# Convolution with max pooling: the input rows of four image pairs as bfloat16 by casting DMA, their row sums by two-input addition, two row differences on VectorE

## The chip, the cores and the metric

The kernel runs on one core of one Trainium2 chip. The metric is the device time of one launch in microseconds. Three runs of the kernel before took 105.48, 104.73 and 104.98 us; the median is 104.98.

A core has five engines that run their own instruction streams and wait for one another by semaphores: TensorE (PE, matrix products, with its weight loads as PEld), VectorE (DVE), ScalarE (ACT), GpSimd (POOL) and SyncE (SP, which here only issues DMAs). SBUF is the working memory of 128 partitions; PSUM is the memory that TensorE writes, here eight banks, each a tile `acc` of 128 x 512 float32.

## What is computed

A convolution of 16 images (64 channels, 64 x 64) with a 3 x 3 kernel to 128 channels, zero padding of one, then the maximum over 2 x 2 windows:

```python
x_pad = np.pad(x, ((0, 0), (0, 0), (pad, pad), (pad, pad)), mode='constant')
...
conv[b, co] += weight[co, ci, kh, kw] * x_pad[b, ci, kh:kh+h, kw:kw+w]
...
output[b, c, i, j] = np.max(conv[b, c, i*pool_size:(i+1)*pool_size,
                                      j*pool_size:(j+1)*pool_size])
```

## The kernel before

**Tiles and steps.** Two images lie side by side on the partitions (64 channels each), so there are eight image pairs. A pair is cut into four quarters of 16 rows (8 rows after pooling), which makes 32 steps. Each step is done for both halves, that is for both images; every TensorE operation has a partner on the other half of the array, and the two run side by side. The string `TYPES` gives each step its kind. Steps of kind K (11 of them) read the rows as bfloat16, with five products: two for each of the two output rows of a pooling window, and one on the sum of two input rows (`ks`), which both output rows have in common and which is added after the maximum of the two. Steps of kind W (21) first transform the rows into a row difference `wd` (16 rows), a row difference `we` and a row sum `ws` (8 rows each), and are left with four products; the one on `ws` is added after the row maximum. `place` gives each step its pair and quarter; with the K steps first, steps 3, 4, 6, 8 are the quarters of pair 3, steps 9, 11, 12, 14 those of pair 4, 16, 17, 19, 20 those of pair 5, 22 to 25 those of pair 6 and 27, 28, 30, 31 those of pair 7.

**Operations.** In the order list an operation is named by letters, step and, where it has one, half:
- loads: `L` and `LB` (float32 rows of a W step into one of three tiles `wx`, issued on SP; `LB` also waits for the last two-input operation of VectorE), `LK` (rows of K steps into `kx`, cast to bfloat16 by the DMA, issued on POOL)
- row operations: `KS` (sum for a K step, VectorE), `WS` (`ws`, VectorE), `E` (`we`, POOL, or VectorE for four steps), `D` (`wd`, POOL)
- products on TensorE: `PA1`, `PA2`, `PB1`, `PB2`, `PR` for K steps, `P2` (reads `we`), `P0` and `P3` (read `wd`), `P1` (reads `ws`) for W steps. A product is three matmuls of 512 or 504 columns.
- after the products: `EV` (ScalarE copies the first bank out), `SE` (ScalarE copies it into the second bank), `MX` (rowmax, VectorE), `OD` (ScalarE copies the odd columns), `CM` (colmax, VectorE, which frees the second bank), and then the store on SP.
- at the start: preparation of the weights (`GS`, `GM`, `uGM`, `TGM` and others like them: sums on POOL and VectorE, copies on POOL, transposes on TensorE) and casts of the first K rows (`XOa`, `XEb`, `X1`).

**What sets the order.** The schedule is written out by hand: the text `ORDER` (line 493) lists every operation, and each engine runs its own in that order. Products of the two halves wait in two lanes and are issued in pairs. One rule is added: an operation of POOL (`on_gpsimd`) waits for the last two-input operation on SBUF that VectorE has before it in the order (`on_vector`). `WS` is a two-input addition under that rule, except for the steps in `SUM_BY_REDUCTION` (line 40), where it is a reduction over pairs of rows (line 315) that isn't noted by `on_vector`.

**What the change touches.** `wload` (97) and `late_load` (390) for the loads, `wx_rows` (306) for the tile that a W step reads, `ws` (310) and `wd` (337) for the sums and the 16-row difference. The order list stays the same, among it these parts:

```
... TG1 GS F.2.0 VD2 XOa LB.3 LB.4 LB.6 LB.8 LB.9 GM VG0 F.3.0 XOb F.0.0 uGM ... XEb LK.0.0 ...
... E.11 P1.6.0 D.11 ... WS.9 ... KS.10 ... E.14 ... D.14 E.12 ... WS.11 ... D.12 L.22 L.23 ... D.16 ... WS.14 ...
... WS.16 ... D.17 ... E.17 D.20 E.20 D.19 ... WS.17 ...
```

Of the kernel before, what the change touches and what calls it, by code (L numbers as in the profile page):

```python
# [11 lines left out]
def kernel(  # L12
# [9 lines left out]
    nc = tc.nc  # L22
    FP32 = mybir.dt.float32
    BF16 = mybir.dt.bfloat16
    MAX = mybir.AluOpType.max
    ADD = mybir.AluOpType.add
    SUB = mybir.AluOpType.subtract

    B, CI, H, W = x.shape
# [4 lines left out]
    R = HO // NQ  # L34
# [2 lines left out]
    TYPES = "KWKWWKWKWWKWWKWKWWKWWKWWWWKWWKWW"  # L37
    DIFF_ON_VECTOR = (3, 4, 6, 11,)
    CAST_ON_VECTOR = ()
    SUM_BY_REDUCTION = (1, 3, 9, 11, 12, 14, 16, 17, 19, 20, 22,)  # L40
    N = len(TYPES)
    KSTEPS = [s for s in range(N) if TYPES[s] == "K"]
    WSTEPS = [s for s in range(N) if TYPES[s] == "W"]
# [4 lines left out]
    const = ctx.enter_context(tc.tile_pool(name="const", bufs=1))  # L48
# [18 lines left out]
    sbuf_op = [None]  # L67

    def behind(inst, other):
        if other is not None:  # L70
            tc.add_manual_dep(inst.ins, other.ins.name, SYNC, reason="order")
# [5 lines left out]
    def on_gpsimd(inst):  # L77
        behind(inst, sbuf_op[0])
        return inst


    def rows_of(p, lo, hi):
        return x[2 * p : 2 * p + 2].rearrange("b c h w -> (b c) h w")[:, lo:hi, :]

    def chunk(q):
        return (2 * R * q + (q > 0), min(H, 2 * R * (q + 1) + 1))

    NWX = 3
    kx = {}
    wx = [const.tile([128, H + 2, W], FP32, name=f"wx_{i}") for i in range(NWX)]  # L90

    def kload(p, lo, hi):
        if p not in kx:
            kx[p] = kx_pool.tile([128, H, W], BF16, name="kx")
        return nc.gpsimd.dma_start(out=kx[p][:, lo:hi, :], in_=rows_of(p, lo, hi))  # L95

    def wload(s, part=None):
        p, q = place[s]
        lo, hi = chunk(q)
        if s == WSTEPS[0] and q > 0:  # L100
            lo = 2 * R * q - 1
        if part == 0:
            hi = 2 * R * q + R + 1
        elif part == 1:
            lo = 2 * R * q + R + 1
        return nc.sync.dma_start(out=wx[p % NWX][:, lo + 1 : hi + 1, :], in_=rows_of(p, lo, hi))
# [11 lines left out]
    for s in first_loads:  # L118
        if s == KSTEPS[1]:
            nc.sync.dma_start(out=ksecond, in_=rows_of(0, klo2, khi2))  # L120
        else:
            wload(s, 0)
            wload(s, 1)
# [2 lines left out]
    ident = const.tile([128, 128], BF16)  # L126
    make_identity(nc, ident)
    for t in wx:
        nc.gpsimd.memset(t[:, 0, :], 0.0)
        nc.gpsimd.memset(t[:, H + 1, :], 0.0)  # L130

# [163 lines left out]
    row = {}  # L295
# [9 lines left out]

    def wx_rows(s):
        p, q = place[s]
        return wx[p % NWX], 2 * R * q + 1

    def ws(s):  # L310
        row["ws", s] = ws_pool.tile([128, R, W], BF16, name="ws")
        t, f = wx_rows(s)
        if s in SUM_BY_REDUCTION:
            with nc.allow_low_precision("bf16 operand of TensorE, as the other row sums"):
                nc.vector.tensor_reduce(  # L315
                    out=row["ws", s],
                    in_=t[:, f : f + 2 * R, :].rearrange("p (r two) w -> p r w two", two=2),
                    axis=mybir.AxisListType.X,
                    op=ADD,
                )  # L320
            return
        on_vector(
            nc.vector.tensor_tensor(  # L323
                out=row["ws", s], in0=t[:, f : f + 2 * R : 2, :], in1=t[:, f + 1 : f + 2 * R : 2, :], op=ADD
            )
        )

    def we(s):
        row["we", s] = e_pool.tile([128, R, W], BF16, name="we")
        t, f = wx_rows(s)  # L330
        vector = s in DIFF_ON_VECTOR
        inst = (nc.vector if vector else nc.gpsimd).tensor_tensor(  # L332
            out=row["we", s], in0=t[:, f : f + 2 * R : 2, :], in1=t[:, f + 1 : f + 2 * R : 2, :], op=SUB
        )
        (on_vector if vector else on_gpsimd)(inst)

    def wd(s):
        row["wd", s] = d_pool.tile([128, 2 * R, W], BF16, name="wd")
        t, f = wx_rows(s)
        on_gpsimd(  # L340
            nc.gpsimd.tensor_tensor(  # L341
                out=row["wd", s], in0=t[:, f + 1 : f + 1 + 2 * R, :], in1=t[:, f - 1 : f - 1 + 2 * R, :], op=SUB
            )
        )

    def we_half(part):
        s = WSTEPS[0]
        if part == 0:
            row["we", s] = e_pool.tile([128, R, W], BF16, name="we")
        t, f = wx_rows(s)  # L350
        lo, hi = f + R * part, f + R * (part + 1)
        on_vector(
            nc.vector.tensor_tensor(
                out=row["we", s][:, R // 2 * part : R // 2 * (part + 1), :],
                in0=t[:, lo:hi:2, :],
                in1=t[:, lo + 1 : hi : 2, :],
                op=SUB,
            )
        )
# [16 lines left out]
    def lk(n, part):  # L376
        quarters = min(NQ, NK - n * NQ)
        last = min(H, 2 * R * quarters + 1)
        half = 2 * R * 2 + 1
        if n == 0:  # L380
            inst = kload(0, *chunk(2 + part))
            if part == 0:
                behind(inst, sbuf_op[0])
        elif part == 0:
            kload(n, 0, min(last, half))
        else:
            kload(n, half, last)


    def late_load(s):  # L390
        behind(wload(s), sbuf_op[0])

    ev, od, ot, made = {}, {}, {}, {}

# [58 lines left out]
    def cast_more(first):  # L453
# [27 lines left out]
        "SEa": lambda h: seed_half(0, h),  # L481
        "SEb": lambda h: seed_half(1, h),
        "KS": ks, "WS": ws, "E": we, "D": wd, "L": wload, "LB": late_load, "LK": lk,
        "SE": seed, "EV": evac, "MX": rowmax, "OD": odd, "CM": colmax,
    }
# [108 lines left out]
```

## Time and profile before

The profiled execution has a span of 103.4 us from its first to its last instruction; the page gives no other time of that execution. The mean granted clock of TensorE is 0.993.

| | before |
|---|---|
| median of three runs | 104.98 us |
| span of the profiled execution | 103.4 us |
| ScalarE busy | 82.2 us (79%) |
| `wd` on POOL, line 341 | 20 of 2.36 us |
| `we` on POOL, line 332 | 16 of 1.27 us |
| `ws` by reduction, line 315 | 11 of 1.23 us |
| `ws` by two-input addition on float32, line 323 | 10 of 0.72 us |
| `ks`, two-input addition on bfloat16, line 301 | 11 of 0.43 us |
| casting loads issued on POOL, line 95 | 6 of 0.59 us |
| moved by DMA | 23.33 MB, 226 GB/s on average |

A row of the timeline gives the start in us from the beginning of the span, the duration, the engine, the line of the kernel, the operation, the tiles as written<-read with their shapes, and in brackets how long the engine had been idle before it and what ended that.

### The profile page before, as it was taken

How to read it: one execution, taken by the hardware profiler on the slowest of the kernel's cores; microseconds unless marked ns; L12 is line 12 of the kernel's file. 1: busy time of each engine (PE TensorE's matmuls, PEld its weight loads, DVE VectorE, ACT ScalarE, POOL GpSimd, SP SyncE). 2: the span in 40 equal slices, each digit the busy share in tenths (PEclk: the TensorE clock that was granted, in tenths of full speed). 3: DMA queues.
4: the chain of work that ended last, by engine and by line, in shares of the span. 5: the costliest groups of instructions: out<-in, count | busy, mean ns of one | idle time of the engine just before them, and what ended most of it. 6: DMA issues, size and time to landing. Idle time of an engine off the chain costs nothing.

```text
span 103.4 us, 2541 instructions
## 1 busy us (share of the span) xinstructions
PE 97.2 (94%) x909; PEld 62.9 (61%) x909; DVE 92.0 (89%) x179; ACT 82.2 (79%) x181; POOL 75.6 (73%) x65
## 2 busy tenths in 40 slices
PE   6999799999999999999999999999999999999910
PEld 2497655555865465576666685556746777777600
DVE  1389899999999999999999999999989996979960
ACT  4546988886789997993887898987899898698820
POOL 6046869773995899998999997959997919970000
PEclk9999999999999999999999999999999999999997
DMA  2988999999999999999859992187699232006152
GB/s 62 299 312 262 360 291 268 349 416 404 248 194 298 286 318 339 351 340 204 163 159 261 312 384 101 56 205 263 176 154 257 81 136 101 0 13 233 65 202 102
DMA packets 13341, 23.33 MB, mean 226 GB/s; under 512 B 1040, under 2 KB 9488, under 8 KB 13328
## 3 DMA queue, kind: packets, MB, share of 16 engines
q1 hardware_dynamic: 12320, 20.68, 60.8%
q0 software_dynamic: 864, 2.36, 13.7%
q8 instruction: 7, 0.11, 0.4%
q10 hardware_dynamic: 144, 0.13, 0.4%
q14 instruction: 6, 0.05, 0.1%
HBM read 17.14 MB, written 8.39 MB: 247 GB/s over the span
## 4 chain that ended last, share of the span: by engine, by line
PE 91%; DVE 3%; issue 1%; DVEq 0%
PE acc L200 85%; PE acc L551 3%; PE acc L164 2%; DVE acc L427 2%; DVE o L437 1%; DVEq L589 0%; DVEq L437 0%; DVEq L427 0%
## 5 line engine op out<-in xcount | busy, mean ns | idle before, releaser
L200 PEld LDWEIGHTS <-wt 64*128 64x128 bf16 x876 | 59.6, 94 | 31.5 <-issue 1.5
L341 POOL TENSOR_TENSOR wd<-wx 128x1024 bf16<-128x1024 f32 x20 | 47.1, 2361 | 7.7 <-PE acc L200 3.4
L200 PE MATMUL acc<-wd,wt 64*128 64x504 bf16 (+3 forms) x264 | 50.1, 367 | 0.0
L200 PE MATMUL acc<-kx,wt 64*128 64x504 bf16 (+6 forms) x288 | 50.0, 356 | 0.0
L427 DVE TENSOR_TENSOR acc<-acc,ev 128x512 f32<-128x512 f32 x64 | 42.0, 691 | 1.1 <-ACT ev L401 0.3
L200 PE MATMUL acc<-we,wt 64*128 64x512 bf16 (+2 forms) x132 | 31.7, 367 | 0.0
L200 PE MATMUL acc<-ws,wt 64*128 64x504 bf16 (+1 forms) x126 | 28.7, 377 | 0.1
L401 ACT ACTIVATE ev<-acc 128x512 f32<-128x512 f32 x42 | 25.1, 608 | 2.7 <-PE acc L200 2.3
L431 ACT COPY od<-acc 128x256 f32<-128x256 f32 x64 | 22.5, 379 | 5.8 <-PE acc L200 5.2
L437 DVE TENSOR_TENSOR o<-acc,od 128x256 f32<-128x256 f32 x64 | 24.5, 416 | 2.1 <-ACT od L431 1.9
L411 ACT COPY acc<-acc 128x512 f32<-128x512 f32 x40 | 23.0, 581 | 3.0 <-PE acc L200 1.7
L332 POOL TENSOR_TENSOR we<-wx 128x512 bf16<-128x512 f32 x16 | 20.2, 1273 | 3.3 <-DVE ws L323 2.4
L200 PE MATMUL acc<-ks,wt 64*128 64x504 bf16 (+1 forms) x66 | 16.5, 377 | 0.5 <-DVE acc L427 0.5
L315 DVE TENSOR_REDUCE ws<-wx 128x512 bf16<-128x1024 f32 x11 | 13.5, 1229 | 0.0
L399 ACT COPY ev<-acc 128x512 f32<-128x512 f32 x22 | 12.9, 595 | 0.6 <-PE acc L200 0.6
L323 DVE TENSOR_TENSOR ws<-wx 128x512 bf16<-128x512 f32 x10 | 7.1, 723 | 0.0
L301 DVE TENSOR_TENSOR ks<-kx 128x512 bf16<-128x512 bf16 x11 | 4.6, 429 | 0.3 <-ACT kx L458 0.3
L551 PE MATMUL acc<-const-bfloat16-1.0 128*128 128x512 bf16 x8 | 3.6, 628 | 0.8 <-PEq L575 0.8
L95 POOL DMA_DIRECT2D kx<-in_x_dram x6 | 3.5, 587 | 0.7 <-DVE kx L451 0.7
L164 PEld LDWEIGHTS <-wq 128*128 128x128 bf16 x25 | 2.3, 132 | 1.4 <-issue 1.4
L151 POOL COPY wq<-wq 128x64 bf16<-128x64 bf16 x3 | 0.7, 241 | 3.1 <-ACT wq L462 2.5
L164 PE MATMUL acc<-ident,wq 128*128 128x128 bf16 x25 | 2.8, 285 | 0.0
(30 smaller groups left out, 22.3 us busy)
## 6 DMA issues: line engine op xcount, KB each, us to landing
out_dram<-o SPq DMA_DIRECT2D x31, 256.0 KB, 4.2
wx<-in_x_dram SPq DMA_DIRECT2D x10, 512.0 KB, 7.2
wx<-in_x_dram SPq DMA_DIRECT2D x5, 544.0 KB, 7.6
wx<-in_x_dram SPq DMA_DIRECT2D x5, 480.0 KB, 7.4
kx<-in_x_dram POOLq DMA_DIRECT2D x2, 528.0 KB, 7.4
ksecond<-in_x_dram SPq DMA_DIRECT2D x1, 512.0 KB, 7.0
kx<-in_x_dram POOLq DMA_DIRECT2D x2, 256.0 KB, 7.0
kx<-in_x_dram POOLq DMA_DIRECT2D x1, 496.0 KB, 12.0
```

The costliest lines, as they stand in the source:

```text
L164: nc.tensor.transpose(tp[:, (j - lo) * CO : (j - lo + 1) * CO], wq[:, j : j + 2, :].rearrange("a b c -> a (b c)"), ident,)
L200: nc.tensor.matmul(acc[t][:, i0:i1, o0:o1], wt[lo : lo + CI, tap_of(m0, kw, h), :], rows(lo, i0, i1, c0, c1), start=start and kw == 1, sto ...
L315: nc.vector.tensor_reduce(out=row["ws", s], in_=t[:, f : f + 2 * R, :].rearrange("p (r two) w -> p r w two", two=2), axis=mybir.AxisListTy ...
L323: nc.vector.tensor_tensor(out=row["ws", s], in0=t[:, f : f + 2 * R : 2, :], in1=t[:, f + 1 : f + 2 * R : 2, :], op=ADD)
L332: inst = (nc.vector if vector else nc.gpsimd).tensor_tensor(out=row["we", s], in0=t[:, f : f + 2 * R : 2, :], in1=t[:, f + 1 : f + 2 * R : ...
L341: nc.gpsimd.tensor_tensor(out=row["wd", s], in0=t[:, f + 1 : f + 1 + 2 * R, :], in1=t[:, f - 1 : f - 1 + 2 * R, :], op=SUB)
L399: nc.scalar.copy(out=ev[s, h], in_=acc[t])
L401: nc.scalar.mul(ev[s, h], acc[t], -1.0)
L411: nc.scalar.copy(out=acc[t], in_=acc[ta[s, h]])
L427: nc.vector.tensor_tensor(out=t, in0=t, in1=ev[s, h], op=MAX)
L431: nc.scalar.copy(out=od[s, h], in_=acc[tb[s, h]][:, :, 1::2])
L437: nc.vector.tensor_tensor(out=ot[s][:, h], in0=acc[t][:, :, 0::2], in1=od[s, h], op=MAX)
```

## The change

The W steps of pairs 4 to 7 read their rows from four new bfloat16 tiles `wb`, one for each pair, instead of the three float32 tiles `wx`. Two quarters are loaded at once, by one casting DMA on POOL's queue, where the first of the two stands in the order list; the second's entry in the list does nothing. So sixteen loads on SP become eight on POOL: those of `LB.9`, `L.12`, `L.16`, `L.19`, `L.22`, `L.24`, `L.27` and `L.30`. Two rows of each new tile are zeroed at the start by POOL. The nine row sums of these pairs that were reductions become two-input additions, noted by `on_vector`; the two of pair 2 and pair 3 (steps 1 and 3) stay reductions. The 16-row differences of steps 12 and 19 move from POOL to VectorE, at their places in the list.

```diff
-    SUM_BY_REDUCTION = (1, 3, 9, 11, 12, 14, 16, 17, 19, 20, 22,)
+    SUM_BY_REDUCTION = (1, 3,)
+    TAPS_ON_VECTOR = (12, 19,)
+    FIRST_BF16 = 4
...
+    wb = {
+        p: const.tile([128, H + 2, W], BF16, name=f"wb_{p}") for p in range(FIRST_BF16, B // 2)
+    }
...
     def wload(s, part=None):
         p, q = place[s]
+        if p in wb:
+            if q % 2:
+                return None
+            lo, hi = chunk(q)[0], chunk(q + 1)[1]
+            return nc.gpsimd.dma_start(out=wb[p][:, lo + 1 : hi + 1, :], in_=rows_of(p, lo, hi))
...
+    for t in wb.values():
+        nc.gpsimd.memset(t[:, 0, :], 0.0)
+        nc.gpsimd.memset(t[:, H + 1, :], 0.0)
...
     def wx_rows(s):
         p, q = place[s]
-        return wx[p % NWX], 2 * R * q + 1
+        return wb.get(p, wx[p % NWX]), 2 * R * q + 1
...
     def wd(s):
         row["wd", s] = d_pool.tile([128, 2 * R, W], BF16, name="wd")
         t, f = wx_rows(s)
-        on_gpsimd(
-            nc.gpsimd.tensor_tensor(
-                out=row["wd", s], in0=t[:, f + 1 : f + 1 + 2 * R, :], in1=t[:, f - 1 : f - 1 + 2 * R, :], op=SUB
-            )
+        vector = s in TAPS_ON_VECTOR
+        inst = (nc.vector if vector else nc.gpsimd).tensor_tensor(
+            out=row["wd", s], in0=t[:, f + 1 : f + 1 + 2 * R, :], in1=t[:, f - 1 : f - 1 + 2 * R, :], op=SUB
         )
+        (on_vector if vector else on_gpsimd)(inst)
...
     def late_load(s):
-        behind(wload(s), sbuf_op[0])
+        inst = wload(s)
+        if inst is not None:
+            behind(inst, sbuf_op[0])
```

## The prediction

> **What bounds the kernel now.** I read the busy shares first, then the chain of waits, then the table by stretches of time, and last the timelines of VectorE (DVE), GpSimd (POOL), TensorE (PE) and the DMA issues around each step that the change touches.
>
> ```profile
> PE 97.2 (94%) x909; PEld 62.9 (61%) x909; DVE 92.0 (89%) x179; ACT 82.2 (79%) x181; POOL 75.6 (73%) x65
> PE 91%; DVE 3%; issue 1%; DVEq 0%
> 11.03 64.89 PE acc L200 x609
> 75.94 20.43 PE acc L200 x186
> 40.00:50.00 10.00, 10.00 (x96) 6.50 (x93) 10.00 (x18) 7.62 (x18) 9.50 (x7) 1.00 0.97 289
> ```
>
> The chain of waits is TensorE alone from 11.03 to 96.37: 795 matmuls in 85.3 us, two side by side every 0.215 us, at a granted clock of 1.00. In the last row (PE, PEld, DVE, ACT, POOL busy, then clock, DMA share, GB/s) VectorE is as full as TensorE, and the DMA engines are full too. So less work on VectorE wins nothing by itself, while anything that reaches TensorE late is paid in full. And the order was cut close: colmax CM.9.1 ends at 39.33 and the matmul that needs its PSUM bank starts at 39.45; D.3 ends at 16.16 and its first matmul starts at 16.25. Through the middle the bank that a colmax frees is taken up 0.05 to 0.7 us later, again and again (end of each colmax in VectorE's timeline against the start of the matmul that the bank order gives it).
>
> **The change, part by part.**
>
> *VectorE's own work falls.* Nine reductions of 1.23 us (L315) become two-input sums on bfloat16; the nearest row is L301, the same shape on bfloat16, at 0.43: 9 x 0.80 = 7.2 us. The seven two-input sums on the bfloat16 pairs go from 0.68 to 0.43: 1.8 us. D.12 and D.19 come to VectorE: twice the elements of L301's 0.43. L437 with 256 elements takes 0.42 and L332 with 512 takes 0.68, so 512 more cost up to 0.53 in f32, or half of that if bfloat16 runs at twice the rate, as L301 against L332 suggests: 0.70 to 0.96 each. I take 0.70, the row of the same type. Net -7.6 us of 92.0. At nothing for the end, since TensorE is full.
>
> *POOL* loses two operations of 2.36 us (L341), gains eight DMA issues at 0.54 to 0.70 (L95), some 4.6 us, and eight memsets at the start, which run every 0.09 us: 0.7 us, covered by its wait of 2.52 us at 4.79. Whether its operations get shorter on bfloat16 no row shows; between 2.36 and half of it, I take 2.36. SP loses sixteen loads.
>
> *Where the sums meet POOL.* This is the first cost. The timelines of the two engines show what happens when a VectorE operation with two SBUF inputs is issued while POOL runs one:
>
> ```profile
> 67.76 1.27 POOL L332 TENSOR_TENSOR we<-wx 128x512 bf16<-128x512 f32 x1 [0.51 <-DVE ks L301]
> 68.72 0.87 DVE L323 TENSOR_TENSOR ws<-wx 128x512 bf16<-128x512 f32 x1
> 69.67 4.68 POOL L341 TENSOR_TENSOR wd<-wx 128x1024 bf16<-128x1024 f32 x2 [0.63 <-DVE ws L323]
> 74.03 0.86 DVE L323 TENSOR_TENSOR ws<-wx 128x512 bf16<-128x512 f32 x1
> 37.78 1.23 DVE L315 TENSOR_REDUCE ws<-wx 128x512 bf16<-128x1024 f32 x1
> ```
>
> The sum at 68.72 ends 0.56 after POOL's operation (69.03), the one at 74.03 ends 0.54 after it (74.35), L301's at 67.03 0.28 after it (67.25): VectorE stands still until POOL is done, then streams (0.55 us in f32, 0.28 in bfloat16). The reduction at 37.78 runs under a POOL operation (37.09 to 39.46) at its usual 1.23. So a sum that now falls under POOL's operation waits for that operation's end, and VectorE's queue behind it (rowmax, colmax, which free PSUM banks) waits too. On the other side, POOL's operations are ordered behind the last two-input VectorE operation, so each new one adds a wait to POOL. In the times of before:
> - WS.9 (34.16): D.11 holds POOL to 35.45; end 35.73 for 35.39, 0.34 late.
> - WS.11: E.14 started 0.25 later behind KS.10, D.14 ends at 39.70, the sum at 39.98 for 39.00: 1.0 late. CM.9.1 is next and had 0.11: TensorE stands 0.9.
> - D.12 adds 0.6 to VectorE: 1.6 late. D.16 now waits for it, 42.1 to 44.45. WS.14 comes at 42.75 and ends at 44.73 for 42.34: 2.4 late. WS.12 meets no operation and wins back 0.8. Colmax CM.10.1, whose bank had 0.24, is 1.6 late: TensorE's loss is 1.4.
> - WS.16 wins 0.8 back, but D.17 waits for it: 50.5 for 47.54. So E.17 ends at 54.1 and D.20 follows. D.19, at VectorE's turn at 54.0, waits for E.17, ends at 54.7; WS.17 right behind it waits for D.20 (54.7 to 57.05) and ends at 57.35 for 54.27: 3.1 late. The next colmax, CM.13.0, had 0.28: TensorE's loss is 2.8.
> - From WS.20 on the sums are short, POOL no longer has D.19, and VectorE catches up; TensorE can't.
>
> Who goes first when POOL has a second operation queued (E.12 behind D.14, D.20 behind E.17) no row shows: always VectorE gives 1.4, always POOL about 4.1 (WS.17 at 58.7). I take 2.8, the alternation.
>
> *The loads at the start.* This is the second cost. Today pair 4's first rows are LB.9, the last of five loads issued on SP from 6.95. The change makes them one casting load of 33 rows, twice as large, on POOL's queue ahead of LK.0.0: after gsum, 6.77 to about 7.4. uGM then starts at 7.45 for 7.40, which the transposes at 8.12 hide.
>
> ```profile
> q1 hardware_dynamic: 12320, 20.68, 60.8%
> q0 software_dynamic: 864, 2.36, 13.7%
> 8.00:13.00 5.00, 4.46 (x71) 3.40 (x69) 4.59 (x10) 4.19 (x11) 3.97 (x5) 1.00 0.94 312
> 13.00:20.00 7.00, 7.00 (x70) 3.68 (x66) 6.79 (x13) 6.17 (x15) 5.44 (x3) 1.00 1.06 294
> 13.02 0.69 DVE L332 TENSOR_TENSOR we<-wx 128x512 bf16<-128x512 f32 x1
> 13.80 4.67 POOL L341 TENSOR_TENSOR wd<-wx 128x1024 bf16<-128x1024 f32 x2 [1.14 <-DVE we L332]
> 16.25 0.38 PE L200 MATMUL acc<-wd,wt 64*128 64x512 bf16 x1
> ```
>
> The casting queue's 2.36 MB are bfloat16, so 4.72 MB read, in 13.7% of 16 x 103.4 us: 48 us of one DMA engine for each MB, as for the plain queue (48.6). So casting saves no DMA time, and the 1.08 MB of this load take 1.08 x 48 / 16 = 3.2 us of all engines, in a stretch whose DMA share is 0.94 to 1.06. Two steps wait there. LB.3, issued at 6.95, landed 6.0 later at 12.95, and E.3 reads it at 13.02; D.3 follows, and its matmul at 16.25 had 0.09. LB.3 comes later by between 0 (the older load wins) and 3.2 (the new load goes between); issued within half a microsecond of each other, I take the half, 1.6: TensorE stands 1.5. LK.0.0, now behind the new load in one queue, landed 9.0 after 8.32, at 17.3, for the matmuls at 18.21; later by 0 to 3.2, I take 2.4, since all of the new load is ahead of it: 19.7, also 1.5 after its need. The two don't add, since a stand at 16.25 moves 18.21 as well. LK.0.1 (12.09 + 8.4 = 20.5, used at 20.6) moves with them. LK.0.0 today, issued by 9.02, landed behind LB.4 (7.32 + 7.1 = 14.4) though LB.4 was long under way, which speaks for something near the order of issue. The Trainium skill (DMA: Bandwidth & Descriptors, Queues, rings and completion order) says that a DMA engine takes turns between its queues, packet by packet. By that LB.3 would bear nearly the whole 3.2 and the sum would be 1.6 higher, as in the last rival below.
>
> Later casting loads are needed over 10 us after their issue, and stores that wait beside them hold output tiles, of which there are six; both at nothing. A step takes TensorE 85.3 / 32 = 2.7 us, so a tile comes round after 16 us, and a store that took 8 more than its median of 4.2 would still be in time.
>
> *Sum.* 1.5 + 2.8 = 4.3 us on the profiled execution's span of 103.4. The page gives that execution no time of its own; the median of the runs, 104.98, is 1.6 us above its span, and I leave these 1.6 as they are: 109.3.
>
> **The rivals.**
> - *One of the two costs is hidden.* For it: the new load may queue behind LB.3, or VectorE may get its turn each time. Against: both spots have under 0.3 us. It gives 104.98 + 1.5 to 2.8: 106.5 to 107.8. A POOL that runs bfloat16 in half the time belongs here: D.14 and D.20 then hold VectorE 1.2 us less, leaving about 1 us in the middle: 107.5. The Trainium skill (GPSIMD Engine Reference, Elementwise — side-by-side cycle accounting) counts cycles for each element, not byte, which would keep 2.36; no row here can show it.
> - *VectorE's 7.6 us cover it all, not slower.* Sums with their 0.8 us won run ahead of POOL instead of under it, and loads land in the order of issue. It decides if VectorE is nowhere over 0.3 us late at a colmax: 105.0. Against: the first sums, WS.9 and WS.11, fall under POOL operations that are already running, before anything is won.
> - *Faster by over 1%.* It would need TensorE to save more than the 0.54 us that it idles at 11.03 and the 1.1 of issue in the chain: about 104. Nothing in the change shortens a matmul.
> - *Every turn goes to POOL and the new load goes first*: 3.1 + 4.1: 112.2.
>
> **How the numbers follow.** This kernel can tell about 1% from no change. Both costs 0.45; one hidden 0.27; all hidden 0.12; faster 0.04; every turn to POOL 0.12. Slower is 0.45 + 0.27 + 0.12 = 0.84. The range leaves out the worst of the last case and most of the two that are not slower: 105.4 to 112.2.
>
> **What would show it.** Right: a wait of TensorE between 14 and 21 us that ends with wd or kx, E.3 starting after 14; sums at L323 of 1 to 3 us instead of 0.43 where POOL runs; POOL waiting for ws more often than its five times now. Wrong: TensorE's row of busy x96 in every ten microseconds as before, the sums all at 0.43, the reads of pair 3 landing by 13.0.

## The result and the profile after

| | before | after |
|---|---|---|
| median of the runs on the same chip | 105.05 us (104.73 to 105.48, 4 runs) | 110.73 us (109.57 to 111.59, 4 runs) |
| ratio, 95% interval | | 1.053 [1.044, 1.061] |
| span of the profiled execution | 103.4 us | 109.8 us |

The change makes the kernel slower by 5.7 us. The profiled execution of after took 111.59 us, the longest of its four; its steps are therefore compared below with those of other kernels that contain the same parts.

Busy shares and the chain of waits (share of the span by engine), from the page of after:

```profile
PE 97.7 (89%) x909; PEld 57.2 (52%) x909; DVE 90.3 (82%) x181; ACT 81.9 (75%) x181; POOL 71.9 (65%) x79
PE 46%; DVE 5%; issue 1%; ACT 1%; DVEq 0%; ACTq 0%
```

TensorE does the same 909 matmuls in nearly the same 97.7 us, in a span 6.4 us longer. The chain that ended last is no longer TensorE from end to end. Its pieces in order of time (start, us, what), from 47.46 on:

```profile
47.46 0.58 ACT acc L427
...
48.08 11.84 PE acc L214 x107
...
59.96 0.27 DVE ws L337
...
60.85 0.70 DVE acc L443
...
61.59 39.09 PE acc L214 x358
```

TensorE's row is broken twice, by ScalarE's copy into a bank at 47.46 and by a row sum and a rowmax of VectorE at 60. The waits of TensorE (total us, times, longest) name a third place:

```profile
PE acc L214 <- DMA kx<-in_x_dram: 3.1, 1, 3.1
PE acc L214 <- DVE acc L443: 2.2, 2, 1.6
PE acc L214 <- ACT acc L427: 1.1, 1, 1.1
```

To size these places I set the start of each product matmul of after against the same matmul of before. The lateness grows at three matmuls only (each growth is counted from the level that it had after the one before), and by the last matmul (98.30 before, 104.55 after) it is 6.25 us:

| matmul | before | after | lateness grows by | what it waits for |
|---|---|---|---|---|
| PA1.5, first half | 18.21 | 21.32 | 3.3 (from 0.17 early) | LK.0.0, landed at 21.27 |
| P0.12, second half | 43.38 | 48.08 | 1.59 | SE.12 on ScalarE, which waited for a colmax queued behind WS.14 |
| PR.15, second half | 55.06 | 61.59 | 1.83 | MX.15.1 on VectorE, queued behind D.19 and WS.17 |

The last two in the stretches of time (us, busy time and count of PE, PEld, DVE, ACT, POOL, then clock, DMA share, GB/s):

```profile
44.00:48.00 4.00, 2.94 (x27) 1.21 (x24) 4.00 (x8) 2.19 (x6) 2.64 (x2) 1.00 0.87 105
56.00:62.00 6.00, 4.38 (x42) 2.76 (x39) 5.60 (x8) 3.68 (x8) 5.49 (x4) 1.00 0.72 183
```

TensorE works 2.94 of four and 4.38 of six microseconds there. VectorE counts as busy almost throughout, as before; how much of that is standing still, only the durations show. The timeline of POOL and VectorE around the two places:

```profile
39.87 2.12 POOL L355 TENSOR_TENSOR wd<-wb 128x1024 bf16<-128x1024 bf16 x1
40.85 1.42 DVE L337 TENSOR_TENSOR ws<-wb 128x512 bf16<-128x512 bf16 x1
41.95 1.33 POOL L346 TENSOR_TENSOR we<-wb 128x512 bf16<-128x512 bf16 x1
44.64 2.11 POOL L355 TENSOR_TENSOR wd<-wb 128x1024 bf16<-128x1024 bf16 x1 [0.84 <-DVE wd L355]
44.99 2.05 DVE L337 TENSOR_TENSOR ws<-wb 128x512 bf16<-128x512 bf16 x1
...
53.18 0.41 DVE L337 TENSOR_TENSOR ws<-wb 128x512 bf16<-128x512 bf16 x1
53.77 2.12 POOL L355 TENSOR_TENSOR wd<-wb 128x1024 bf16<-128x1024 bf16 x1 [3.44 <-DVE ws L337]
...
56.97 2.12 POOL L355 TENSOR_TENSOR wd<-wb 128x1024 bf16<-128x1024 bf16 x1
57.73 1.91 DVE L355 TENSOR_TENSOR wd<-wb 128x1024 bf16<-128x1024 bf16 x1
59.05 1.59 POOL L346 TENSOR_TENSOR we<-wb 128x512 bf16<-128x512 bf16 x1
59.56 1.36 DVE L337 TENSOR_TENSOR ws<-wb 128x512 bf16<-128x512 bf16 x1
```

The sum of 53.18, which meets no operation of POOL, takes 0.41. WS.11 (40.85) takes 1.42 and ends 0.28 after D.14; WS.14 (44.99) takes 2.05 and ends 0.28 after D.16; D.19 (57.73) ends 0.55 after D.20. And D.17 (53.77) has waited 3.44 for a sum on VectorE. This is the stand that the prediction took from three rows of before.

The start, by the DMA issues at 6 to 9 us of after (KB, us from issue to landing), the first being LB.3, then pair 4's first load, then LK.0.0:

```profile
wx<-in_x_dram SPq DMA_DIRECT2D x1, 544.0 KB, 4.8
wb<-in_x_dram POOLq DMA_DIRECT2D x1, 528.0 KB, 10.3
...
kx<-in_x_dram POOLq DMA_DIRECT2D x1, 256.0 KB, 13.3
```

LK.0.0 took 9.0 before and takes 13.3 now. LB.3 took 6.0 and takes 4.8: it is not hurt at all.

### The profile page after: what moved, and what is told of

It reads as the page before. It is cut to its first block, busy times and chain, and to the rows that moved or that the text cites. A ratio compares the mean times of both kernels' runs of the same rounds, so it can differ in the third digit from the quotient of the medians.

```text
span 109.8 us, 2528 instructions
## 1 busy us (share of the span) xinstructions
PE 97.7 (89%) x909; PEld 57.2 (52%) x909; DVE 90.3 (82%) x181; ACT 81.9 (75%) x181; POOL 71.9 (65%) x79
## 4 chain that ended last, share of the span: by engine, by line
PE 46%; DVE 5%; issue 1%; ACT 1%; DVEq 0%; ACTq 0%
PE acc L214 46%; DVE acc L443 3%; DVE o L453 2%; ACT acc L427 1%; DVEq L605 0%; DVE ws L337 0%; DVEq L443 0%; DVEq L453 0%; ACTq L427 0%
## 5 line engine op out<-in xcount | busy, mean ns | idle before, releaser
L214 PEld LDWEIGHTS <-wt 64*128 64x128 bf16 x876 | 54.1, 94 | 43.4 <-issue 5.3
L355 POOL TENSOR_TENSOR wd<-wb 128x1024 bf16<-128x1024 bf16 x14 | 29.7, 2123 | 11.0 <-DVE ws L337 5.5
L346 POOL TENSOR_TENSOR we<-wb 128x512 bf16<-128x512 bf16 x15 | 17.8, 1191 | 4.2 <-PE acc L214 2.1
L337 DVE TENSOR_TENSOR ws<-wb 128x512 bf16<-128x512 bf16 x16 | 10.8, 682 | 0.0
L355 POOL TENSOR_TENSOR wd<-wx 128x1024 bf16<-128x1024 f32 x4 | 9.4, 2351 | 1.7 <-DVE we L346 1.7
L109 POOL DMA_DIRECT2D wb<-in_x_dram x8 | 4.7, 585 | 0.9 <-DVE kx L467 0.9
L346 POOL TENSOR_TENSOR we<-wx 128x512 bf16<-128x512 f32 x1 | 1.3, 1266 | 4.7 <-DVE ws L337 4.7
```

Of the source, the lines that this page charges most:

```text
L109: return nc.gpsimd.dma_start(out=wb[p][:, lo + 1 : hi + 1, :], in_=rows_of(p, lo, hi))
L214: nc.tensor.matmul(acc[t][:, i0:i1, o0:o1], wt[lo : lo + CI, tap_of(m0, kw, h), :], rows(lo, i0, i1, c0, c1), start=start and kw == 1, sto ...
L337: nc.vector.tensor_tensor(out=row["ws", s], in0=t[:, f : f + 2 * R : 2, :], in1=t[:, f + 1 : f + 2 * R : 2, :], op=ADD)
L346: inst = (nc.vector if vector else nc.gpsimd).tensor_tensor(out=row["we", s], in0=t[:, f : f + 2 * R : 2, :], in1=t[:, f + 1 : f + 2 * R : ...
L355: inst = (nc.vector if vector else nc.gpsimd).tensor_tensor(out=row["wd", s], in0=t[:, f + 1 : f + 1 + 2 * R, :], in1=t[:, f - 1 : f - 1 + ...
```

## The experiments

Each edit is against the kernel after. "Ratio" is to the kernel before on the same chip, with its 95% interval.

| run | median us | before | ratio |
|---|---|---|---|
| e1_loads_only | 108.18 | 104.59 | 1.030 [1.022, 1.037] |
| e2_vector_only | 114.75 | 104.59 | 1.095 [1.089, 1.100] |
| e3_load_later | 108.23 | 104.59 | 1.033 [1.027, 1.038] |
| e4_later_old_sums | 104.94 | 104.59 | 1.0025 [0.9997, 1.0053] |
| e5_later_sums_only | 106.45 | 104.81 | 1.015 [1.010, 1.021] |
| e6_later_taps_only | 106.62 | 104.81 | 1.017 [1.012, 1.023] |
| e7_one_quarter | 108.51 | 104.81 | 1.037 [1.032, 1.043] |
| e8_load_between | 109.49 | 104.81 | 1.045 [1.039, 1.052] |
| e9_three_reductions | 106.81 | 105.03 | 1.017 [1.011, 1.023] |
| e10_two_quarters | 109.35 | 105.03 | 1.042 [1.038, 1.045] |
| e11_sums_not_noted | 107.15 | 105.03 | 1.021 [1.017, 1.024] |
| e12_free_sums | 105.13 | 105.03 | 1.0026 [0.9995, 1.0056] |

**Only the loads.** The sums and differences go back to what they were; the bfloat16 loads stay.

```diff
-    SUM_BY_REDUCTION = (1, 3,)
-    TAPS_ON_VECTOR = (12, 19,)
+    SUM_BY_REDUCTION = (1, 3, 9, 11, 12, 14, 16, 17, 19, 20, 22,)
+    TAPS_ON_VECTOR = ()
```

> The bfloat16 loads alone: the nine sums stay reductions and both differences stay on GpSimd. Theory of two separate costs (the casting load ahead of LK.0.0 at the start, about 3.3 us in the profile; two-input sums and differences that meet GpSimd's operations in the middle, about 3.4 us): 108.3 us, with TensorE waiting at PA1.5 near 18 to 21 us and nowhere in the middle. Rival, casting loads hurt all along: 110 us or more, with waits in the middle too. Rival, only VectorE against GpSimd costs, and the late landing was chance: 105 us.

Measured: 1.030. The waits of its TensorE:

```profile
PE acc L214 <- DMA kx<-in_x_dram: 2.2, 1, 2.2
PE acc L567 <- PEq L591: 0.8, 1, 0.8
PE acc L214 <- DVE acc L443: 0.5, 1, 0.5
```

The start's wait is there (LK.0.0 landed at 20.42, PA1.5's lateness grew by 2.4) and both steps of the middle are gone. The start costs about 3% alone.

**Only VectorE's part.** All rows stay float32 on their old loads; the sums are two-input and D.12 and D.19 are on VectorE.

```diff
-    FIRST_BF16 = 4
+    FIRST_BF16 = 8
```

> The VectorE part alone, on float32 rows loaded as before: nine sums by two-input addition, D.12 and D.19 on VectorE. Two costs: no loss at the start, and in the middle at least the 3.4 us of the changed kernel, since the operations are longer in float32 (0.55 against 0.28 us for a sum, some 1.2 against 0.7 for a difference, 2.36 against 2.12 on GpSimd): 108.5 to 111 us. Rival, all of the loss comes from the loads: 105 us.

Measured: 1.095, well beyond what was expected. The start's step is gone, but this isn't the middle part alone: float32 operations of POOL and VectorE are longer, so each stand is longer (D.19 took 3.35, WS.14 2.54), and one stand of TensorE was long enough to lose its clock (last section). It shows that on float32 rows the sums and the differences together cost far more; for the price of the middle in this change the next run is the cleaner one.

**The load behind LK.0.1.** Pair 4's first load is issued after LK.0.0 and LK.0.1 instead of ahead of them; nothing else changes.

```diff
-        LB.8 LB.9 GM VG0 F.3.0 XOb F.0.0 uGM F.1.0 VG1 F.0.1 TGM PA2.2.1 XEb LK.0.0 F.1.1 F.2.1 F.3.1 VGM GP
+        LB.8 GM VG0 F.3.0 XOb F.0.0 uGM F.1.0 VG1 F.0.1 TGM PA2.2.1 XEb LK.0.0 F.1.1 F.2.1 F.3.1 VGM GP
...
-        LK.0.1 X2 PR.0.0 G.1.0 X1 G.2.0 PB1.2.1 PB2.2.1 WS.1 G.2.1 G.1.1 L.11 P0.3.1 PA1.2.0 PA2.2.0 P3.3.1
+        LK.0.1 LB.9 X2 PR.0.0 G.1.0 X1 G.2.0 PB1.2.1 PB2.2.1 WS.1 G.2.1 G.1.1 L.11 P0.3.1 PA1.2.0 PA2.2.0 P3.3.1
```

> The changed kernel with its first casting load (LB.9) moved behind LK.0.1 on GpSimd's queue. Two costs: the wait at PA1.5 is gone, the two steps in the middle stay, 107.4 us. Rival, the start's loss is no matter of the order of these two loads: 110.7 us as the changed kernel. Rival, the middle's loss only follows from the start's: below 106 us.

Measured: 1.033, 108.23 us, 0.8 above the expected 107.4. Its TensorE waits for VectorE and ScalarE and for no load:

```profile
PE acc L214 <- DVE acc L443: 2.1, 2, 1.6
PE acc L214 <- ACT acc L427: 1.1, 1, 1.1
```

LK.0.0 landed at 17.22 and the start's step is gone. P0.12 and PR.15 lose 1.59 and 1.85, as in after. So the two costs come apart: 3.0% and 3.3% alone, 5.3% [4.4, 6.1] together, which is their sum within the intervals of the three.

**Both taken away.** The previous edit, and the old reductions and POOL's differences as in the first run. All loads still cast.

> Casting loads with LB.9 moved behind LK.0.1, and sums and differences as before the change: both suspected costs are taken away and only the casting loads are left. Two costs: 105.0 us, within 0.5 us of the kernel before. Rival, casting loads cost by themselves (issue on GpSimd, stores that wait longer): 106 us or more. Shorter GpSimd operations on bfloat16 (2.12 against 2.36 us) should win nothing, since TensorE is full.

Measured: 1.0025, no difference. The busy shares:

```profile
PE 96.9 (94%) x909; PEld 54.5 (53%) x909; DVE 89.6 (87%) x179; ACT 82.1 (80%) x181; POOL 75.0 (73%) x81
```

TensorE is back at 94%. Casting sixteen loads in eight on POOL's queue costs nothing once LK.0.0 and LK.0.1 are not behind one of them. A reduction under POOL's operation, from its timeline, is not held:

```profile
52.75 1.15 POOL L346 TENSOR_TENSOR we<-wb 128x512 bf16<-128x512 bf16 x1
52.78 1.21 DVE L329 TENSOR_REDUCE ws<-wb 128x512 bf16<-128x1024 bf16 x1
```

**Sums or differences alone.** The load is late in both. The first keeps the two-input sums and has `TAPS_ON_VECTOR = ()`; the second keeps the differences on VectorE and has the old `SUM_BY_REDUCTION`.

> As e3 (first casting load behind LK.0.1), but D.12 and D.19 stay on GpSimd: the nine two-input sums alone. If each sum that falls under a GpSimd operation holds VectorE until that ends, WS.11, WS.14, WS.12 and WS.17 still wait, each 0.5 to 2 us: 106.5 to 107.5 us, TensorE's first loss again between 38 and 48 us. Rival, the two moved differences (2 x 0.7 us and their waits) are what costs: 105 us.

> As e3, but the nine sums stay reductions: D.12 and D.19 on VectorE alone. D.12 adds 0.6 us to a full VectorE with 0.1 to 0.3 us to spare, D.19 waits for the GpSimd operation that runs at its turn, up to 1.2 us: 105.3 to 106.5 us. Rival, the differences carry the whole loss of e3: 108.2 us.

Measured: 1.015 and 1.017 (106.45 and 106.62 us, each at the edge of what was expected), whose excesses add up to the 3.3% of both. The sums alone cost in four small steps of 0.25 to 0.46, at PR.10, PR.15 and P2.19 among others; the sums held longest were WS.12 (2.09) and WS.17 (1.86). The differences alone cost 0.53 at P0.12 and 1.19 at PR.15, where D.19 took 1.43 for the 0.67 of D.12. I had looked for the first loss of the sums at 38 to 48 us, and it is one of the small ones (PR.10, at 45.6).

**Half the load in front.** Pair 4's first load takes one quarter only, at its old place; the other quarters are loaded one by one where the list has them.

```diff
-            if q % 2:
+            if p > FIRST_BF16 and q % 2:
                 return None
-            lo, hi = chunk(q)[0], chunk(q + 1)[1]
+            lo, hi = chunk(q)
+            if p > FIRST_BF16:
+                hi = chunk(q + 1)[1]
```

> The changed kernel with its first casting load cut to one quarter (17 rows, half the bytes) at LB.9's place, the other quarter at L.11's. If LK.0.0 is late because the whole of the load ahead of it in its queue has to pass first, half the bytes make it half as late: it lands near 19.2 instead of 21.3, TensorE's wait at PA1.5 is 1.0 to 1.6 us instead of 3.3, and the time is 109.2 us. Rival, a casting load issued early costs a fixed delay: 110.7 us.

Measured: 1.037, near e3. LK.0.0 landed at 17.49, in time; the two steps of the middle stay (1.49 and 1.84). I had expected 19.2 and a wait.

**The load between LK.0.0 and LK.0.1.** `LB.9` stands right behind `LK.0.0` in the list.

> The changed kernel with LB.9 between LK.0.0 and LK.0.1. If the order inside GpSimd's queue decides, LK.0.0 lands as before (near 17), PA1.5 doesn't wait, and LK.0.1 lands some 3 us late, so that TensorE waits at PA1.7 near 21 us instead: about 110.5 us. Rival, the transfers share the DMA engines whatever their order, and LK.0.0 is late as well, by half of its 4 us.

Measured: 1.045. LK.0.0 landed at 17.13, in time, and now LK.0.1 is the late one: 22.49, with a step of 1.5 at PA1.7, the first matmul that reads it. What is hurt is whatever stands behind the new load in POOL's queue. I had expected about 3 us of wait there.

**Two loads of half the size in front.** Same bytes at the same place, in two DMAs of a quarter each.

```diff
             lo, hi = chunk(q)[0], chunk(q + 1)[1]
+            if s == 9:
+                lo2, hi2 = chunk(q + 1)
+                nc.gpsimd.dma_start(out=wb[p][:, lo + 1 : lo2 + 1, :], in_=rows_of(p, lo, lo2))
+                lo = lo2
```

> The changed kernel with the first casting load cut into two DMAs of one quarter each, both at its old place ahead of LK.0.0: the same bytes in packets of half the size. If the bytes ahead of LK.0.0 decide, it lands at 20.4 to 21.3 as in the changed kernel, 110.5 us. If the packet size does (in turns with the plain loads, a packet of 8.4 KB read takes twice the time of theirs), it lands near 19 and the time is 109 to 109.5 us, and pair 3's plain loads land earlier than in the changed kernel.

Measured: 1.042 by the median, and a step of 0.9 at PA1.5 instead of 3.3, since LK.0.0 landed at 18.83. The total fits the theory of packet sizes, but two things speak against it as the whole cause. Pair 3's plain loads, which were to land earlier than in after, landed 0.9 to 1.7 later, all but the last (1.0 earlier). And LK.0.0's gain is in part an earlier start. The first casting packet came at 9.43, in after at 10.87, which is 1.4 of the 2.4 us won. From the first packet to LK.0.0's landing it took 9.4 here, 10.4 in after and 9.6 in e1, which has the packets of after. Packet size is worth between 0.2 and 1.0 us, not settled.

**Three reductions back.** e3 with steps 11, 14 and 17 as reductions, `SUM_BY_REDUCTION = (1, 3, 11, 14, 17,)`.

> As e3, but the three sums that waited longest for GpSimd before TensorE's two losses (WS.11, WS.14, WS.17) are reductions again, which don't wait. If the waits themselves cost, WS.14 alone is 0.8 us shorter (1.23 for 2.05) and the loss at P0.12 falls from 1.6 to about 0.8 us, the one at PR.15 from 1.85 to about 1.5: 106.8 to 107.4 us. Rival, what costs is the extra work of D.12 and D.19 on VectorE alone: 108.2 us as e3.

Measured: 1.017, with steps of 0.51 at P0.12 and 1.67 at PR.15. In time that is the differences-alone run again (1.017; 0.53 and 1.19): without the three held sums, what is left is mainly the price of D.12 and D.19. The 0.5 more at PR.15 goes with the sum of step 16, which is still noted here: D.17 waits 3.41 for it, and D.19 takes 1.91 instead of 1.43.

**Sums that POOL doesn't wait for.** e3, but the nine sums aren't noted by `on_vector`, so that POOL's operations are no longer ordered behind them. They still meet POOL.

```diff
-        on_vector(
-            nc.vector.tensor_tensor(
-                out=row["ws", s], in0=t[:, f : f + 2 * R : 2, :], in1=t[:, f + 1 : f + 2 * R : 2, :], op=ADD
-            )
+        inst = nc.vector.tensor_tensor(
+            out=row["ws", s], in0=t[:, f : f + 2 * R : 2, :], in1=t[:, f + 1 : f + 2 * R : 2, :], op=ADD
         )
+        if s not in (9, 11, 12, 14, 16, 17, 19, 20, 22):
+            on_vector(inst)
```

> As e3, but GpSimd's operations don't wait for the nine sums: only VectorE's waits for GpSimd are left. If GpSimd's late start (D.17 waits 3.4 us for WS.16) is what puts D.20 in the way of D.19, the loss at PR.15 goes and the time is 106.6 us. Rival, the waits only change sides, since sums then meet GpSimd operations that run earlier: 107.5 to 109 us.

Measured: 1.021, between the theories. P0.12's 1.59 stays, so the order behind the sums has no part in that one; WS.14 is held for 2.05 as before, under a D.16 that still waits 0.83 for D.12. PR.15's 1.85 falls to 0.57, with another 0.45 at P1.17: 0.8 to 1.3 of it came from the order behind the sums, D.17 waiting for WS.16 and everything of POOL behind it moving under D.19 and WS.17.

**Only the sums that met nothing.** e3 with the sums of steps 16, 19, 20 and 22 as two-input additions, the rest reductions, and the differences on POOL.

```diff
-    SUM_BY_REDUCTION = (1, 3,)
-    TAPS_ON_VECTOR = (12, 19,)
+    SUM_BY_REDUCTION = (1, 3, 9, 11, 12, 14, 17,)
+    TAPS_ON_VECTOR = ()
```

> Casting loads with LB.9 behind LK.0.1, both differences on GpSimd, and two-input addition only for the four sums that met no GpSimd operation in e3 (steps 16, 19, 20, 22): VectorE is relieved and nowhere held. Two costs, TensorE full: 104.9 us, within 0.5 us of the kernel before, no gain from 3.2 us less on VectorE. Rival, VectorE was a second limit and a relief of it wins: below 104.0 us. Rival, GpSimd's longer waits cost: 105.5 us or more.

Measured: 1.0026, no difference, with VectorE relieved:

```profile
PE 97.2 (94%) x909; PEld 54.1 (52%) x909; DVE 88.3 (85%) x179; ACT 82.2 (79%) x181; POOL 75.5 (73%) x81
```

VectorE works 88.3 us instead of 92.0, and the time doesn't move. It wasn't quite "nowhere held": two of the four sums met POOL in the new places, WS.20 (0.75) and WS.22 (1.24), and P2.19 lost 0.5, which the time doesn't show. A sum that is free in one version need not be free in the next. No version here beats the kernel before.

## Why the prediction was right, and where its sizes were off

The forecast of 109.3 us was 1.4 below the 110.7 measured, within its range, and the two costs it named are the two that the experiments took away one by one.

**TensorE is full, so less work on VectorE wins nothing.** Right, and shown by e12 (VectorE busy 3.7 us less) and e4 (2.4 less): both at TensorE's 94% and at the time of before.

**The cost of each operation.** A free sum takes 0.41 (0.43 forecast), D.12 took 0.67 (0.70). POOL's differences are neither unchanged nor halved on bfloat16. The groups of the page of after (busy, mean ns, then idle before and what ended it):

```profile
L355 POOL TENSOR_TENSOR wd<-wb 128x1024 bf16<-128x1024 bf16 x14 | 29.7, 2123 | 11.0 <-DVE ws L337 5.5
...
L337 DVE TENSOR_TENSOR ws<-wb 128x512 bf16<-128x512 bf16 x16 | 10.8, 682 | 0.0
L355 POOL TENSOR_TENSOR wd<-wx 128x1024 bf16<-128x1024 f32 x4 | 9.4, 2351 | 1.7 <-DVE we L346 1.7
```

2.12 on bfloat16, 2.35 on float32: a tenth less, near the end I took. The sums' mean of 0.68 is the 0.41 of the free ones with the stands of the others in it, and POOL's idle time of 5.5 before `wd` is the added order.

**The middle: 2.8 forecast, 3.4 measured (1.59 and 1.83).** The mechanism is right: e4 takes the stands away and the loss with them. Taking alternation between the two bounds was right too: in the rows of 39.87 to 41.95 VectorE's WS.11 goes when D.14 ends, with POOL's E.12 queued (E.12 takes 1.33 instead of 1.14), and at 57 to 61 D.20, D.19, E.20 and WS.17 take turns (E.20 takes 1.59 for 1.15). Single steps of the listing were off. WS.11 was to make TensorE stand 0.9 at CM.9.1 and did not: in e3, where nothing is late before, it ends at 39.23 for a forecast 39.98, since D.14, 0.24 shorter on bfloat16 like all of POOL's 16-row differences, ended at 38.95 instead of 39.70. The first loss came through ScalarE's SE.12, which waited for the bank of a colmax behind WS.14, and not through CM.10.1's own bank. D.19 was held by D.20, not by E.17, and WS.17 by E.20. So the size came out near although two of its terms had another place, and that much is luck. The first term was 1.59 for 1.4. The second, set down as 1.4 (2.8 less 1.4), was 1.83, of which e11 puts 0.8 to 1.3 down to the order added to POOL.

**The start: 1.5 forecast, 2.4 (e1) to 3.3 (after) measured.** The place and the culprit are right (e1, e3, e8), but half the step failed: LB.3 was not late, and E.3, whose start after 14 was to be a sign, started at 12.84. Up to there e1 and after run the same instructions, so the 0.9 between them is spread between executions. The new load's first packet came at 10.87, 3.5 us after its issue ended, and by 11.21 LB.3 had landed. The term that was mis-sized is LK.0.0's: 2.4 later, with 3.2 as the upper bound, forecast; 4.0 later in after (17.28 to 21.27) and 3.1 in e1. The bound itself was wrong: after exceeds it, and e1 stays under it only because its first casting packet came 1.8 earlier than before (10.79 for 12.60). 3.2 us is the new load's time if all engines serve it alone. They don't; the packets of the two queues in 12 to 13 us of after (packets, MB written, share of 16 engines):

```profile
q0 software_dynamic: 34, 0.14, 70.5%
q1 hardware_dynamic: 34, 0.14, 35.5%
```

One packet of the one queue for one of the other, and nearly so in the three microseconds that follow (34 to 31, 44 to 43, 55 to 57). The load that stands ahead of LK.0.0 has only 0.70 of the engines, and 3.2 / 0.70 = 4.6, an estimate from these rows. From the first casting packet to LK.0.0's landing the times are 4.7 with nothing ahead (before), 7.7 with half the load (e7), 9.6 and 10.4 with all of it (e1, after): 4.9 to 5.7 more. The queue starting 1.7 earlier (10.87 for 12.60) takes some of it back. For e7 the same working, with the queue's share of 0.53 there, gives 1.6 / 0.53 = 3.0, and 3.0 was measured; for e10 it gives 5.6 at its mean share of 0.57, and 4.7 was measured, so it is not the whole account. The Trainium skill (DMA: Bandwidth & Descriptors, Queues, rings and completion order) states this turn by turn between queues, packet by packet; the trace agrees, with 34 packets to 34. What I had drawn from it, that LB.3 would bear the 3.2, needed the two to be on their way at once, and in after they were not. In e10 they were: the first casting packet came at 9.43, LB.3 landed at 12.94, 1.7 later than in after, and P2.3 lost 0.57 of a start that was 0.83 early.

**What was put at nothing.** The eight memsets and the eight casting issues in place of SP's sixteen loads: e4 has them all and costs nothing. Stores that took up to 9.1 us to land cost nothing there either.

**The rivals.** "One cost hidden" and "all hidden" are what e1, e3 and e4 show once a cost is removed; in the change neither was. "Every turn to POOL" fell by the rows above. Faster fell with the result, and with e12 also for a relief of VectorE alone.

What stays open: why the engines finish LK.0.0 so unevenly (its packets run from 14.55 to 20.63 in after), and so what packet size is worth.

## What to carry to other kernels

Before replacing an operation by a shorter one, ask what it can be made to wait for: a one-input reduction of 1.23 us that nothing holds up was worth more here than a two-input sum of 0.41 us that becomes 1.0 to 2.05 where it falls under a GpSimd operation. Before moving a load to another queue, list what is behind it there and when that is needed; the same load behind the two that were needed first cost nothing. And bytes ahead in one's own queue cost more than their share of all engines, since the other queue takes its turns meanwhile.

## What the runs showed of the hardware

- A two-input VectorE operation and POOL's take turns operation by operation when both have more queued: neither engine went twice in the rows above. The Trainium skill (SBUF — State Buffer, Who interferes with whom) says that a VectorE instruction with two SBUF inputs contends with a GpSimd instruction that reads SBUF, and that the contention is an exclusive lock; the ends at 0.28 and 0.55 us after POOL's agree.
- The first packet of a casting load came 2.4 to 3.6 us after the issue ended while the plain loads of the start were under way (9.02 to 12.60 before, 7.41 to 10.87 after, 7.43 to 9.83 in e7), and 0.9 us after it later in the kernel (38.51 to 39.37 in after).
- A stand of TensorE can cost more than itself. In e2 TensorE stood from 58.97 to 62.42, from its timeline:

```profile
62.42 0.37 PE L214 MATMUL acc<-ks,wt 64*128 64x512 bf16 x1 [3.45 <-DVE acc L443]
```

and the granted clock (the third number from the end) then fell, in its stretches of time:

```profile
63.00:64.00 1.00, 1.00 (x12) 0.54 (x8) 1.00 (x3) 0.41 (x2) 1.00 (x2) 0.88 0.01 4
64.00:65.00 1.00, 1.00 (x8) 0.42 (x6) 1.00 (x3) 0.75 (x2) 0.47 (x1) 0.50 0.15 54
65.00:66.00 1.00, 1.00 (x8) 0.47 (x6) 0.96 (x4) 0.53 (x2) 0.00 (x0) 0.50 1.08 380
66.00:67.00 1.00, 1.00 (x7) 0.36 (x4) 0.60 (x2) 0.55 (x1) 0.17 (x1) 0.50 0.31 108
67.00:68.00 1.00, 1.00 (x12) 0.53 (x10) 0.00 (x0) 0.49 (x2) 1.00 (x1) 0.92 0.70 245
```

Three microseconds at 0.50, and the two beside them in part, cost about 1.6 us more. The stand of 3.10 us in after left the clock at 1.00. The Trainium skill (TensorE: Matmul & The Clock Gate, What's actually happening) puts the fall to half rate after an idle window of about 3.4 us; the two stands agree with that.
